# q, k and one more pair of gate chunks by Strassen's seven products, beside the attention

## The chip, the cores and the metric

The kernel runs on one core of one Trainium2 chip. A core has five engines, each with its own instruction stream: TensorE (PE, matmuls; PEld in a profile is its weight load), VectorE (DVE), ScalarE (ACT), GpSimd (POOL) and SyncE (SP, which here only issues DMAs). SBUF is the memory on chip with 128 partitions; PSUM has eight banks of 128 x 512 float32, into which TensorE accumulates. The metric is the device time in microseconds (us) of one execution.

## The reference, cut to what matters

One decoder layer for 256 rows of width 2048, 16 heads of 128 and a feed-forward width of 5632, all float32:

```python
h = rmsnorm(x, g_mix)
proj = h @ w_in                      # q, k, v of 16 heads (3 x 2048), then 3 x 2048 gate columns
q, k, v = ...
gates = sigmoid(proj[..., 3 * MIX_WIDTH:])
o_a = stick_breaking_attention(q[:, :4], k[:, :4], v[:, :4])
qn, kn = rmsnorm(q[:, 4:], q_gain), rmsnorm(k[:, 4:], k_gain)
o_b = moba_attention(qn[:, :6], kn[:, :6], v[:, 4:10], rel_bias)
o_c = dilated_attention(qn[:, 6:], kn[:, 6:], v[:, 10:], rel_bias)
merged = gates[0] * (o_a @ w_branch[:512]) + gates[1] * (o_b @ w_branch[512:1280]) \
       + gates[2] * (o_c @ w_branch[1280:])
x = x + merged @ w_out
gu = rmsnorm(x, g_ffn) @ w_gu
x = x + (silu(gu[..., :D_FF]) * gu[..., D_FF:]) @ w_down
```

With 256 rows, MoBA is causal softmax over one block, and the dilated attention is a softmax with a table of biases; so both are `softmax_pair` in the kernel.

## The kernel before

**Precision.** Every large product is done in three matmuls of a faster 32-bit format: a value is split into hi (ScalarE's copy, line 95) and lo (VectorE's subtraction, line 96), and `product` (149 to 152) adds hi*hi, hi*lo and lo*hi. Activations stand as columns of 128 x 128 (the stationary side), weights stream 512 columns wide. A block of weights, `w_raw` or `g_raw`, is two K tiles of 128 by 512 columns, 512 KB, and is split into `w_hi` and `w_lo`, of which there are four buffers each.

**A plain chunk** (`project`, 131) multiplies all 16 K tiles of h by 512 columns, for both row halves, into two PSUM banks `ps`.

**A pair** (`project_pair`, 301) does two chunks, colA and colB. In two of the four K chunks (`WC`) it uses Strassen's scheme: rows, K tiles and the two chunks each make the halves of a 2 x 2 block product, and `form` makes one of seven products, from sums of blocks of h (made once, `put_sums`) and of blocks of the weights (`u`, `add_into`, on VectorE). The other two K chunks are multiplied plainly (`rest`). It holds four PSUM banks: X and Y (`ps`), Z and V (from a second pool `acc2`). Results are put together with `snapshot` (ScalarE) and VectorE. `begin_pair` loads and splits the first blocks of the next pair while the present one ends.

**The order of the work.** h is made from x in `rest_of_x` while the first chunk runs. For each group of four heads q, k and v are three plain chunks, and the group's attention runs in the next group's chunks. This interleaving is by generators: `stages` and `slow_stages` hold functions that yield, and `advance` lets the first in the list do its next step; `project` advances both every second K tile, `parts` (a split in a pair) advances `stages`. `finish_stages` runs a list to its end. Behind the heads come twelve gate chunks: four plain, then four pairs, for which the attention's PSUM banks are given up and the sums of h are made (`sums_of_h`). Then w_branch, w_out, eleven pairs of w_gu, and w_down, whose pairs have their own code. Within each engine a planner of the framework fixes the order of instructions before the run, by a simulated timeline in which earlier program order has precedence; `keep_in_program_order` binds an instruction to the written order (all weight loads of pairs, on SP's queue, among others).

**What the softmax heads do:** q and k are scaled by the first norm (line 616), squared and summed per head on VectorE (619, 620), normalised (583), transposed (590 and following); the scores get the bias (542, 544), which stands in SBUF for all twelve heads, loaded once from a table `vec` in HBM (469).

Of the kernel before, what the change touches and what calls it, by code (L numbers as in the profile page):

```python
# [18 lines left out]
P = 128  # L19
# [36 lines left out]
def hybrid_block(ctx: ExitStack, tc: tile.TileContext, x, g_mix, w_in, q_gain, k_gain, w_branch, w_out,  # L56
# [7 lines left out]
    acc = ctx.enter_context(tc.tile_pool(name="acc", bufs=4, space=PSUM))  # L64
# [16 lines left out]
    hp_stack, h2_stack, ph1, pright = ExitStack(), ExitStack(), ExitStack(), ExitStack()  # L81
# [49 lines left out]
    def project(acts, k0, w, row0, nk, col0, fine=False, last=1):  # L131


        ps = [acc.tile([P, NB], F32, name="ps") for _ in range(NT)]
# [131 lines left out]
    def load(w, k, col0, pl=None):  # L266

        raw = pl.tile([P, 2, NB], F32, name="g_raw", bufs=8 if pl is gx else 4) if pl else wpool.tile([P, 2, NB], F32, name="w_raw", bufs=4)
        (nc.sync.dma_start if w is w_down else fetch)(raw, w[k * P:(k + 2) * P, col0:col0 + NB].rearrange("(k p) n -> p k n", p=P))
        return raw  # L270

    def parts(src):
# [3 lines left out]
        advance(stages)  # L276
        return hi, lo

# [12 lines left out]
    def begin_pair(acts, w, colA, colB):  # L291
# [6 lines left out]
        return p11, b12, u  # L298

    def project_pair(acts, w, colA, colB, begun=None, nxt=None):  # L300
# [23 lines left out]
        p11, b12, u = begun or begin_pair(acts, w, colA, colB)  # L324
# [50 lines left out]
    o = Columns(p1, "o", NH)  # L375
    h = Columns(pool(hp_stack, "hp", "left"), "h", KT)

    pa = pool(pat, "pa", "left", 2)
    zeros = pa.tile([P, NB], F32R, name="zeros", bufs=1)
# [33 lines left out]
    for t in range(NT):  # L413
        to_h(h, xs[0][t], 0, t, g1)
    idle(4)

    def rest_of_x():
        for c in range(1, 4):
            for t in range(NT):
# [5 lines left out]
        for c in range(4):  # L425
            squares(xs[c], ss1, c)
# [4 lines left out]
    stages.append(rest_of_x())  # L431
# [13 lines left out]
    oh_sb = pa.tile([N_BUCKETS, NDIST], F32, name="oh_sb", bufs=1)  # L445
    nc.gpsimd.dma_start(oh_sb, onehot)
    ex_sb = pa.tile([H_SOFT, NDIST], F32, name="ex_sb", bufs=1)
    nc.gpsimd.dma_start(ex_sb, extra)
    rb_sb = pa.tile([N_BUCKETS, H_SOFT], F32, name="rb_sb", bufs=1)
    nc.gpsimd.dma_start(rb_sb, rel_bias)  # L450
    bias = pa.tile([P, H_SOFT, S], F32, name="bias", bufs=1)

    def parameters():
# [7 lines left out]
        yield  # L461
        pb = tr.tile([P, 4 * P], F32, name="tr")
        nc.tensor.matmul(pb[:H_SOFT, :NDIST], rb_sb, oh_sb, start=True, stop=True)
        nc.vector.tensor_add(ex_sb, ex_sb, pb[:H_SOFT, :NDIST])
        vec = dram.tile([H_SOFT, NDIST], F32, name="vec")
        nc.gpsimd.dma_start(vec, ex_sb)
        yield
        for h in range(0, H_SOFT, 4):
            nc.gpsimd.dma_start(bias[:, h:h + 4, :], bass.AP(tensor=vec.tensor, offset=vec.offset + h * NDIST,
                                                             ap=[[1, P], [NDIST, 4], [1, S]]))  # L470
            yield
# [15 lines left out]
    def finish(h0, po):  # L487
        split(o.hi[:, h0:h0 + 2, :], o.lo[:, h0:h0 + 2, :], po)

    def stick_breaking(hl, qT, kT, v):  # L490
# [11 lines left out]
        sp = pa.tile([P, n], F32, name="sb_sp", bufs=1)  # L502
        nc.vector.scalar_tensor_tensor(sp, z[:, :n], 0.0, l, op0=ALU.max, op1=ALU.add)
        lb = pa.tile([P, n], F32, name="sb_lb", bufs=1)
# [27 lines left out]
    def softmax_pair(h0, hl, qT, kT, v):  # L532
        hs = h0 - H_A
# [3 lines left out]
        for i in range(2):  # L537
# [5 lines left out]
                             s[:, 0:W0].rearrange("p (h k) -> p h k", h=2), bias[:, hs:hs + 2, :])  # L543
        nc.vector.tensor_add(p[:, W0:n].rearrange("p (h k) -> p h k", h=2),
                             s[:, W0:n].rearrange("p (h k) -> p h k", h=2), bias[:, hs:hs + 2, P:S])
# [13 lines left out]
        pTs = []  # L559
        for i in range(2):  # L560
# [4 lines left out]
            pT = pa.tile([P, 3 * P], F32, name="sm_pT")  # L565
            nc.scalar.copy(pT.rearrange("p (b q) -> p b q", b=3),
                           backwards(pt[:, :3 * P].rearrange("p (b q) -> p b q", b=3)))
            pTs.append(pT)
# [10 lines left out]
    def rows_to_columns(g, j, sbs, dst, rr):  # L579
        for t in range(NT):  # L580
            if g:
                sb3 = sbs[t].rearrange("p (h d) -> p h d", h=4)
                nc.vector.tensor_mul(sb3, sb3, rr[:, 4 * t:4 * t + 4, None].to_broadcast([P, 4, HD]))
        yield
        yield
        for t in range(NT):
            yield
            pt = transpose4(sbs[t])
            d = dst[:, :, t * P:(t + 1) * P]
# [5 lines left out]
            else:  # L595
                nc.scalar.activation(d, pt, AF.Copy, scale=SCALE)

    def attention(g, qT, kT, v):
        for hl in (0, 2):
            if g:  # L600
                yield from softmax_pair(4 * g + hl, hl, qT, kT, v)
# [4 lines left out]
    for g in range(4):  # L606
        v = pa.tile([P, NT, NB], F32, name="v")
        qkT = [pa.tile([P, 4, S], F32, name=f"{n}T") for n in "qk"]
        for j in range(2):
            ps = project(h, 0, w_in, 0, KT, j * NH * HD + g * NB, fine=g + j == 0)  # L610
            finish_stages(stages)
            ss = pa.tile([P, 4 * NT], F32, name="ss")
            sbs = []
            for t in range(NT):
                sb = half_kb()
                nc.scalar.activation(sb, ps[t], AF.Copy, scale=rstd[:, t:t + 1])
                if g:
                    junk = half_kb()
                    nc.vector.tensor_mul(junk, sb, sb)
                    nc.vector.tensor_reduce(ss[:, 4 * t:4 * t + 4], junk.rearrange("p (h d) -> p h d", h=4),  # L620
                                            op=ALU.add, axis=AX.X)
                sbs.append(sb)
            rr = pa.tile([P, 4 * NT], F32, name="rr")
            if g:
                rsqrt_mean(rr, ss, HD, 4 * NT)
            stages.append(rows_to_columns(g, j, sbs, qkT[j], rr))
        ps = project(h, 0, w_in, 0, KT, 2 * NH * HD + g * NB)
        finish_stages(stages)
        finish_stages(slow_stages)
        for t in range(NT):  # L630
            nc.scalar.activation(v[:, t, :], ps[t], AF.Copy, scale=rstd[:, t:t + 1])
        slow_stages.append(attention(g, *qkT, v))


    gate_mem = dram.tile([3, 4, NT, P, NB], F32, name="gate_mem")

    def gate_col(c, b):
        return 3 * NH * HD + b * D + c * NB
# [7 lines left out]
    def sums_of_h(hs):  # L646
        for c in WC:
            w = gx.tile([P, 4, S], F32, name="u")
            k = slice(4 * c, 4 * c + 4)
            nc.vector.tensor_add(w, h.hi[:, k, :].bitcast(F32), h.lo[:, k, :].bitcast(F32))  # L650
            yield
            hs.put_sums(c, w[:, :, 0:P], w[:, :, P:S], w)
            yield

    chunks = [(c, b) for c in range(4) for b in range(3)]
    for c, b in chunks[:3]:
        keep_gate(c, b, project(h, 0, w_in, 0, KT, gate_col(c, b)))
    finish_stages(slow_stages)
    pat.close()

    acc2 = ctx.enter_context(tc.tile_pool(name="acc2", bufs=1, space=PSUM))
    pg2 = ExitStack()
    hs = Both(pool(pg2, "spg", "left"), h, WC)
    gx = pool(pg2, "gxg", "left", 3)
    stages.append(sums_of_h(hs))
    ps = project(h, 0, w_in, 0, KT, gate_col(*chunks[3]))
    ahead = begin_pair(hs, w_in, gate_col(*chunks[4]), gate_col(*chunks[5]))
    keep_gate(*chunks[3], ps)
    finish_stages(stages)
    for i in range(4, len(chunks), 2):  # L670
        one, two = chunks[i:i + 2]
        nxt = [(hs, w_in, *(gate_col(*cb) for cb in chunks[i + 2:i + 4]))] if i + 2 < len(chunks) else [None]
        g, ahead = project_pair(hs, w_in, gate_col(*one), gate_col(*two), ahead, *nxt)
        keep_gate(*one, g[:2])
        keep_gate(*two, g[2:])
    pg2.close()
    hp_stack.close()


# [244 lines left out]
```

## Time and profile before

| | |
|---|---|
| median of three executions | 1481.12 us (1481.09 to 1482.36) |
| the profiled execution | 1482.6 us, span 1480.8 us |
| mean granted TensorE clock | 0.997 |
| HBM read, written | 292.65 MB, 16.27 MB |
| first q chunk to the last v chunk | about 11 to 314 us |
| gate chunks | about 314 to 584 us |
| w_branch and w_out | to about 765 us |
| w_gu | to about 1222 us |

The span goes from the first to the last instruction; the execution's time has a little around it. A row of grouped instructions has the line, the engine, the operation, what it writes and reads, the count, then busy microseconds and the mean nanoseconds of one, then the idle time of the engine before them and what ended it. The busy time of TensorE is modelled for overlapping matmuls, so single gaps are read from starts.

### The profile page before, as it was taken

What the parts mean: (1) busy time and instruction counts of PE and PEld (TensorE: products, weight loads), DVE (VectorE), ACT (ScalarE), POOL (GpSimd) and SP (SyncE); (2) the same over time, 40 slices, a digit from 0 to 9 for tenths busy, and PEclk for the clock granted to TensorE, in tenths of its full rate; (3) what the DMA queues carried; (4) which work ended last, traced back from release to release, by engine and by line L of the source; (5) the groups of instructions that cost most, each with busy time, mean ns of one, the idle gap of its engine ahead of it and who ended that gap; (6) DMA issues with size and microseconds to landing.
All of it is one profiled execution on the core that took longest, in us unless ns stands there. A gap on an engine that the chain in (4) does not pass through costs nothing.

```text
span 1480.8 us, 17760 instructions
## 1 busy us (share of the span) xinstructions
PE 1469.1 (99%) x6467; PEld 1183.4 (80%) x6467; DVE 1135.7 (77%) x1228; ACT 817.5 (55%) x973; POOL 70.6 (5%) x130
## 2 busy tenths in 40 slices
PE   8999999999999999999999999999999999999998
PEld 6888888888887778888877888888888888888887
DVE  6457575754688887776779999998999888987675
ACT  5554454445466656344546666666656665664453
POOL 1000000000000001110000000000000000010000
PEclk9999999999999999999999999999999999999999
DMA  7655555556765566876776655566675557677553
GB/s 247 225 170 154 175 170 165 165 169 196 261 224 188 198 242 208 298 233 198 230 253 227 248 196 196 196 232 226 213 242 209 181 186 257 233 262 248 186 171 100
DMA packets 154425, 310.11 MB, mean 209 GB/s; under 512 B 10624, under 2 KB 12240, under 8 KB 154336
## 3 DMA queue, kind: packets, MB, share of 16 engines
q1 hardware_dynamic: 142624, 274.24, 55.5%
q0 software_dynamic: 9952, 32.62, 6.7%
q10 hardware_dynamic: 1760, 2.11, 0.4%
q8 instruction: 51, 0.84, 0.2%
q14 instruction: 38, 0.31, 0.1%
HBM read 292.65 MB, written 16.27 MB: 209 GB/s over the span
## 4 chain that ended last, share of the span: by engine, by line
PE 97%; DVE 1%; ACT 1%; DMA 1%; issue 0%; ACTq 0%; DVEq 0%
PE ps L151 23%; PE ps L152 23%; PE ps L150 23%; PE z L151 4%; PE z L152 4%; PE z L150 4%; PE v L150 3%; PE v L151 2%; PE v L152 2%; PE tr L172 2%; PE tr L150 1%; PE tr L152 1%; PE tr L151 1%; DVE w_lo L96 1%; DMA w_raw<-in_w_in 1%; ACT w_hi L95 0%
## 5 line engine op out<-in xcount | busy, mean ns | idle before, releaser
L96 DVE TENSOR_TENSOR w_lo<-w_raw,w_hi 128x1024 fp32r<-128x1024 f32 (+1 forms) x378 | 459.4, 1217 | 223.9 <-ACT w_hi L95 222.3
L95 ACT CAST w_hi<-w_raw 128x1024 fp32r<-128x1024 f32 (+1 forms) x378 | 394.8, 1046 | 394.7 <-PE ps L152 290.0
L152 PE MATMUL ps<-w_hi,h_lo 128*128 128x512 f32 x800 | 316.3, 396 | 0.0
L151 PE MATMUL ps<-w_lo,h_hi 128*128 128x512 f32 x800 | 316.2, 396 | 0.0
L150 PE MATMUL ps<-w_hi,h_hi 128*128 128x512 f32 x800 | 309.5, 399 | 0.8 <-ACT h_hi L95 0.8
L95 ACT CAST w_hi<-g_raw 128x1024 fp32r<-128x1024 f32 x144 | 150.6, 1049 | 96.7 <-PE ps L152 70.2
L96 DVE TENSOR_TENSOR w_lo<-g_raw,w_hi 128x1024 fp32r<-128x1024 f32 x144 | 173.6, 1223 | 36.1 <-ACT w_hi L95 34.0
L150 PEld LDWEIGHTS ps<-w_hi,h_hi 128*128 128x128 f32 x800 | 150.4, 188 | 36.4 <-ACT h_hi L95 1.5
L152 PEld LDWEIGHTS ps<-w_hi,h_lo 128*128 128x128 f32 x800 | 150.2, 188 | 36.3
L151 PEld LDWEIGHTS ps<-w_lo,h_hi 128*128 128x128 f32 x800 | 150.3, 188 | 35.8 <-DVE gq L459 0.6
L95 ACT CAST w_hi<-u 128x1024 fp32r<-128x1024 f32 x108 | 112.9, 1048 | 60.4 <-DVE u L286 53.5
L96 DVE TENSOR_TENSOR w_lo<-u,w_hi 128x1024 fp32r<-128x1024 f32 x108 | 129.5, 1222 | 14.5 <-ACT w_hi L95 13.9
L286 DVE TENSOR_TENSOR u<-u,g_raw 128x1024 f32<-128x1024 f32 x60 | 70.6, 1219 | 0.0
L150 PE MATMUL ps<-w_hi,o_hi 128*128 128x512 f32 x128 | 50.6, 399 | 0.0
L151 PE MATMUL ps<-w_lo,o_hi 128*128 128x512 f32 x128 | 50.6, 395 | 0.0
L152 PE MATMUL ps<-w_hi,o_lo 128*128 128x512 f32 x128 | 50.6, 395 | 0.0
L150 PE MATMUL ps<-w_hi,m_hi 128*128 128x512 f32 x128 | 50.5, 394 | 0.0
L152 PE MATMUL ps<-w_hi,a_lo 128*128 128x512 f32 x128 | 50.4, 394 | 0.0
L151 PE MATMUL ps<-w_lo,a_hi 128*128 128x512 f32 x128 | 50.4, 394 | 0.0
L152 PE MATMUL ps<-w_hi,m_lo 128*128 128x512 f32 x128 | 49.9, 390 | 0.0
L151 PE MATMUL ps<-w_lo,m_hi 128*128 128x512 f32 x128 | 49.8, 389 | 0.0
L281 ACT COPY sc<-ps 128x512 f32<-128x512 f32 x47 | 27.5, 584 | 38.3 <-PE ps L152 38.3
(307 smaller groups left out, 2433.4 us busy)
## 6 DMA issues: line engine op xcount, KB each, us to landing
w_raw<-in_w_in SPq DMA_DIRECT2D x158, 512.0 KB, 3.7
g_raw<-in_w_gu SPq DMA_DIRECT2D x88, 512.0 KB, 7.1
w_raw<-in_w_gu SPq DMA_DIRECT2D x88, 512.0 KB, 4.5
w_raw<-in_w_down SPq DMA_DIRECT2D x64, 512.0 KB, 4.6
g_raw<-in_w_in SPq DMA_DIRECT2D x32, 512.0 KB, 6.6
w_raw<-in_w_branch SPq DMA_DIRECT2D x32, 512.0 KB, 4.7
w_raw<-in_w_out SPq DMA_DIRECT2D x32, 512.0 KB, 4.7
g_raw<-in_w_down SPq DMA_DIRECT2D x24, 512.0 KB, 5.3
```

The source lines that it names most:

```text
L95: nc.scalar.copy(hi, src)
L96: nc.vector.tensor_sub(lo, src, hi.bitcast(F32))
L150: nc.tensor.matmul(ps, ah, wh, start=start, stop=False, **how)
L151: nc.tensor.matmul(ps, ah, wl, start=False, stop=False, **how)
L152: nc.tensor.matmul(ps, al, wh, start=False, stop=stop, **how)
L172: nc.tensor.transpose(pt[:, i, :], src[:, i * P:(i + 1) * P], ident)
L281: nc.scalar.copy(sb, ps)
L286: tc.keep_in_program_order(nc.vector.tensor_add(d, d, a))
```

## The change: what it does

1. The units of the input projection get a list of their own: v of group 0, gate chunk 0, then q and k of group 0 as one pair, q and k of group 1, v of group 1, and so on; gate chunk 1, then **five** pairs of gates. v and two gate chunks stay plain. Nine pairs of the input projection stand where there were four.
2. PSUM: `acc` has two names, `ps` and `qs`, of two banks each, used in turn (`banks`). A q/k pair takes all four (X, Y of one name, Z, V of the other), since the attention's banks are in use.
3. `wpool` has five buffers of `w_hi` and `w_lo` in place of four; `g_raw` has six in place of eight. `begin_pair` also loads and splits b21.
4. The sums of h are made inside `rest_of_x`, and the squares for the first norm are spread over it. `project` advances `stages` at every K tile; `parts` advances `slow_stages` at every second split.
5. To find the room: the attention's output is kept as float32 (`o_raw`) and split later, during the gate pairs; the bias is loaded per two heads; the tables' inputs go through the scratch pool and are loaded later; two tiles of the attention share a buffer, `v` has one.
6. The squares of q and k move to ScalarE, one instruction per head.
7. Behind: the early tiles of the down stage, its weight buffers and `a_raw` (two buffers) get other places in SBUF; the descriptor ring of POOL's DMAs is 4096 bytes.

```diff
-    acc = ctx.enter_context(tc.tile_pool(name="acc", bufs=4, space=PSUM))
+    acc = ctx.enter_context(tc.tile_pool(name="acc", bufs=2, space=PSUM))
...
-    wpool = pool(ctx, "wpool", "right", 4)
+    wpool = pool(ctx, "wpool", "right", 5)
     scratch = pool(ctx, "scratch", "right", 12)
+    gx = pool(pgx, "gx", "right", 2)
...
+    turn = ["ps", "qs"]
+    def banks():
+        turn.reverse()
+        return [acc.tile([P, NB], F32, name=turn[1]) for _ in range(2)]
...
         for k, w_hi, w_lo in weights(w, row0, nk, col0, fine):
+            if k:
+                advance(stages)
             if k % 2 == 0 and k:
-                advance(stages)
                 advance(slow_stages)
...
-        raw = pl.tile([P, 2, NB], F32, name="g_raw", bufs=8 if pl is gx else 4) ...
+        raw = pl.tile([P, 2, NB], F32, name="g_raw", bufs=6 if pl is gx else 4) ...
...
         split(hi, lo, src)
         advance(stages)
+        split_count[0] += 1
+        if split_count[0] % 2:
+            advance(slow_stages)
...
-        return p11, b12, u
+        b21 = quarter(acts, w, 1, colA)
+        return p11, b12, u, b21, [parts(b) for b in b21]
...
-        X = acc.tile([P, NB], F32, name="ps")
-        Y = acc.tile([P, NB], F32, name="ps")
-        Z = acc2.tile([P, NB], F32, name="z")
-        V = acc2.tile([P, NB], F32, name="v")
+        X, Y = banks()
+        Z, V = others()
...
         s1 = snapshot(X)
-        b21 = quarter(acts, w, 1, colA)
-        form(Y, 2, b21, True, False)
+        form(Y, 2, p21, True, False, True)
...
+    def rest_of_x(columns):
         for c in range(1, 4):
-            for t in range(NT):
-                to_h(h, xs[c][t], c, t, g1)
+            squares(xs[c - 1], ss1, c - 1)
+            hcs = [to_h(h, xs[c][t], c, t, g1) for t in range(NT)]
             if c < 3:
                 xs.append(load_x(c + 1, fetch))
             yield
+            if c - 1 in WC:
+                hs.put_sums(c - 1, *columns)
+            columns = hcs
             yield
...
+        oh_sb, ex_sb, rb_sb = (half_kb() for _ in range(3))
+        nc.gpsimd.dma_start(oh_sb[:N_BUCKETS, :NDIST], onehot)
+        nc.gpsimd.dma_start(ex_sb[:H_SOFT, :NDIST], extra)
+        nc.gpsimd.dma_start(rb_sb[:N_BUCKETS, :H_SOFT], rel_bias)
+        yield
+        yield
         pb = tr.tile([P, 4 * P], F32, name="tr")
...
     def finish(h0, po):
-        split(o.hi[:, h0:h0 + 2, :], o.lo[:, h0:h0 + 2, :], po)
+        nc.scalar.copy(o_raw[:, h0:h0 + 2, :], po)
...
+    def rows_to_columns(g, sbs, dst):
+        if g:
+            ss = pa.tile([P, 4 * NT * 2], F32, name="ss", bufs=1)
+            for i, sb in enumerate(sbs):
+                junk = half_kb()
+                for hd in range(4):
+                    cols = slice(hd * HD, (hd + 1) * HD)
+                    nc.scalar.activation(junk[:, cols], sb[:, cols], AF.Square,
+                                         accum_out=ss[:, 4 * i + hd:4 * i + hd + 1])
+                yield
+            rr = pa.tile([P, 4 * NT * 2], F32, name="rr", bufs=1)
+            rsqrt_mean(rr, ss, HD, 4 * NT * 2)
+            yield
...
     def attention(g, qT, kT, v):
+        biases = []
+        if g:
+            for hl in (0, 2):
+                bias = pa.tile([P, 2, S], F32, name="bias")
+                nc.gpsimd.dma_start(bias, bass.AP(tensor=vec.tensor, ...))
+                biases.append(bias)
...
+    def keep_v(g, ps):
+        finish_stages(slow_stages)
+        heads["v", g] = v = pa.tile([P, NT, NB], F32, name="v", bufs=1)
+        for t in range(NT):
+            nc.scalar.activation(v[:, t, :], ps[t], AF.Copy, scale=rstd[:, t:t + 1])
+        if g:
+            slow_stages.append(attention(g, *heads["qk", g], v))
+
+    def keep_qk(g, q0, q1, k0, k1):
+        sbs = []
+        for t, (src, own) in enumerate(((q0, True), (q1, False), (k0, True), (k1, True))):
+            sb = src if own else half_kb()
+            nc.scalar.activation(sb, src, AF.Copy, scale=rstd[:, t % NT:t % NT + 1])
+            sbs.append(sb)
+        heads["qk", g] = qkT = [pa.tile([P, 4, S], F32, name=f"{n}T") for n in "qk"]
+        if g:
+            stages.append(rows_to_columns(g, sbs, qkT))
+        else:
+            slow_stages.append(rows_to_columns(g, sbs, qkT))
+            slow_stages.append(attention(g, *qkT, heads["v", g]))
...
+    units = [("v", 0), ("gate", chunks[0]), ("qk", 0), ("qk", 1), ("v", 1), ("qk", 2), ("v", 2), ("qk", 3), ("v", 3)]
+    units += [("gate", chunks[1])] + [("gates", chunks[i:i + 2]) for i in range(2, len(chunks), 2)]
...
+    def in_turn():
+        turn.reverse()
+        return [acc.tile([P, NB], F32, name=turn[1]) for _ in range(2)]
+
+    def beside():
+        return [acc2.tile([P, NB], F32, name=n) for n in "zv"]
+
+    def split_o():
+        for k in range(0, NH, 4):
+            split(o.hi[:, k:k + 4, :], o.lo[:, k:k + 4, :], o_raw[:, k:k + 4, :])
+            yield
+            yield
...
+    others = in_turn
+    ahead = None
+    for (kind, what), after in zip(units, units[1:] + [(None, None)]):
+        if kind == "gates" and what[0] == chunks[4]:
+            finish_stages(slow_stages)
+            pat.close()
+            acc2 = ctx.enter_context(tc.tile_pool(name="acc2", bufs=1, space=PSUM))
+            others = beside
+            o = Columns(pool(ph1, "o", "left"), "o", NH)
+            stages.append(split_o())
+        nxt = pair_of(*after)
+        if kind in ("qk", "gates"):
+            ps, ahead = project_pair(*pair_of(kind, what), ahead, nxt)
+            if others is in_turn:
+                turn.reverse()
+        else:
+            ps = project(h, 0, w_in, 0, KT, 2 * NH * HD + what * NB if kind == "v" else gate_col(*what),
+                         fine=(kind, what) == ("v", 0))
+            ahead = begin_pair(*nxt) if nxt else None
+        finish_stages(stages)
...
+    pe = pool(ctx, "pe", "left")
...
+    pr = pool(ctx, "pr", "right")
+    gd = pool(ctx, "gd", "right", 4)
...
-        raw = pe.tile([P, 4, S], F32, name="a_raw", bufs=1)
+        raw = pr.tile([P, 4, S], F32, name="a_raw", bufs=2)
...
-    nc = bacc.Bacc("TRN2", target_bir_lowering=False, num_devices=1)
+    nc = bacc.Bacc("TRN2", target_bir_lowering=False, num_devices=1, dynamic_dma_scratch_size=4096)
```

More of the change, by code (lines that the diff above doesn't have):

```diff
@@ L429, in rest_of_x @@
         rsqrt_mean(rstd, sst, D, NT)
[L431 removed]
+    stages.append(rest_of_x(columns))
     before = pa.tile([P, P], F32, name="before", bufs=1)
@@ L443, in hybrid_block @@
     nc.gpsimd.memset(neg_ones, -1.0)
[L445 to L451, printed above, removed]
+    vec = dram.tile([H_SOFT, NDIST], F32, name="vec")
     def parameters():
@@ L461, in parameters @@
         yield
+        oh_sb, ex_sb, rb_sb = (half_kb() for _ in range(3))
[4 more added lines that the diff above has]
+        yield
         pb = tr.tile([P, 4 * P], F32, name="tr")
[L463 to L466, printed above, removed]
+        nc.tensor.matmul(pb[:H_SOFT, :NDIST], rb_sb[:N_BUCKETS, :H_SOFT], oh_sb[:N_BUCKETS, :NDIST], start=True, stop=True)
+        nc.vector.tensor_add(ex_sb[:H_SOFT, :NDIST], ex_sb[:H_SOFT, :NDIST], pb[:H_SOFT, :NDIST])
+        nc.gpsimd.dma_start(vec, ex_sb[:H_SOFT, :NDIST])
         yield
[L468 to L471, printed above, removed]
     stages.append(parameters())
@@ L658, in hybrid_block @@
[L658 to L675, printed above, removed]
@@ L676, in hybrid_block @@
-    pg2.close()
-    hp_stack.close()
+    others = in_turn
[18 more added lines that the diff above has]
+        finish_stages(stages)
+        if kind == "v":
+            keep_v(what, ps)
+        elif kind == "qk":
+            keep_qk(what, *ps)
+        elif kind == "gate":
+            keep_gate(*what, ps)
+        else:
+            keep_gate(*what[0], ps[:2])
+            keep_gate(*what[1], ps[2:])
```

124 lines of the change are left out of this document (45 added, 79 removed).

## The prediction

> **What bounds the kernel now.** I read the page first: the engines' busy time and the chain that ended last.
>
> ```profile
> PE 1469.1 (99%) x6467; PEld 1183.4 (80%) x6467; DVE 1135.7 (77%) x1228; ACT 817.5 (55%) x973; POOL 70.6 (5%) x130
> PE 97%; DVE 1%; ACT 1%; DMA 1%; issue 0%; ACTq 0%; DVEq 0%
> ```
>
> TensorE (PE) is busy 99% of the span and is 97% of the chain, so a matmul taken away should shorten the run, as long as nothing else becomes late. Next, the busy time by stretch: the start, three groups of four heads (q, k, v chunks with attention in between), one pair of gate chunks, and the w_gu stage.
>
> ```profile
> core 0: us, PE busy (x) PEld busy (x) DVE busy (x) ACT busy (x) POOL busy (x), PEclk, DMA share, GB/s
> 11.00:39.50 28.50, 28.50 (x125) 22.49 (x125) 21.32 (x33) 18.72 (x34) 0.52 (x1) 0.92 0.73 236
> 161.40:237.80 76.40, 76.40 (x354) 62.14 (x353) 48.72 (x77) 37.30 (x59) 0.00 (x0) 1.00 0.56 169
> 498.00:541.00 43.00, 42.61 (x182) 33.72 (x182) 37.63 (x35) 26.95 (x32) 2.24 (x5) 1.00 0.63 221
> 780.00:1222.00 442.00, 442.00 (x1937) 355.36 (x1938) 403.60 (x375) 280.86 (x314) 18.31 (x27) 1.00 0.61 213
> ```
>
> In the group of heads VectorE (DVE) has 27.7 of 76.4 us free. In w_gu, made of Strassen pairs alone, it works 403.6 of 442 us (91%) and TensorE never idles. The waits that TensorE does have come from one source:
>
> ```profile
> PE ps L151 <- DVE w_lo L96: 3.1, 5, 1.9
> PE z L151 <- DVE w_lo L96: 0.5, 3, 0.2
> ```
>
> The unit price of a matmul comes from the chain in order of time (start, length, what), and from single rows of the timeline:
>
> ```profile
> 449.94 0.70 PE ps L150 x3
> 457.45 1.24 DVE w_lo L96
> 462.46 1.06 ACT w_hi L95
> 463.55 1.24 DVE w_lo L96
> 492.86 0.70 PE ps L150 x3
> ...
> 893.63 0.70 PE ps L150 x3
> 936.51 0.70 PE ps L150 x3
> ```
>
> ```profile
> 454.91 0.39 PE L150 MATMUL ps<-w_hi,h_hi 128*128 128x512 f32 x1
> ...
> 457.71 0.39 PE L151 MATMUL ps<-w_lo,h_hi 128*128 128x512 f32 x1
> ```
>
> Three matmuls take 0.70 us on the chain, and twelve lie between starts at 454.91 and 457.71: 2.80 / 12 = **0.2333 us each** (the 0.39 is latency; they overlap). A gate pair recurs after 492.86 - 449.94 = 42.92 us. It has 180 matmuls, 42.0 us, so 0.9 us of it is waiting: the chain leaves TensorE at 457 and at 462 to 464. A w_gu pair recurs after 42.88 us, which eight transposes fill; it waits for nothing.
>
> **The change, part by part.**
>
> **The products.** Two chunks taken plainly are 2 x 16 K tiles x 2 row halves x 3 = 192 matmuls. A pair takes seven products in place of eight in two of four K chunks: 2 x 7 x 2 x 3 = 84, and 96 for the other two, 180. Five pairs are new (q and k of four groups, and one of gates), each replacing two plain chunks: 5 x 12 = 60 matmuls, 60 x 0.2333 = **-14.0 us**. All attention matmuls and transposes remain in number.
>
> The Trainium skill ("TensorE: Matmul & The Clock Gate", section Wait — 56ns, not 53.3ns?) gives 215.7 ns between warm matmuls of 512 columns; by that the saving would be an estimated 12.9 us. The trace's 0.2333 differs from it and I keep the trace.
>
> **What else the pairs ask of VectorE and ScalarE.** Grouped rows of the q/k/v stage (85 to 314 us, three groups): count, then busy us and mean ns of one, then the idle time before and its releaser.
>
> ```profile
> L96 DVE TENSOR_TENSOR w_lo<-w_raw,w_hi 128x1024 fp32r<-128x1024 f32 x73 | 89.4, 1224 | 69.0 <-ACT w_hi L95 69.0
> L619 DVE TENSOR_TENSOR sc<-sc 128x512 f32<-128x512 f32 x12 | 8.3, 688 | 3.1 <-ACT sc L616 3.1
> L620 DVE TENSOR_REDUCE ss<-sc 128x4 f32<-128x512 f32 x12 | 8.2, 685 | 0.3
> L95 ACT CAST w_hi<-w_raw 128x1024 fp32r<-128x1024 f32 x72 | 75.4, 1048 | 95.1 <-PE ps L152 93.7 <-issue 1.0
> L553 ACT ACTIVATE p<-p,sm_st 128x128 f32<-128x128 f32 x8 | 3.1, 388 | 0.0
> L553 ACT ACTIVATION_READ_ACCUMULATOR p<-p,sm_st 128x1 f32 x16 | 3.0, 187 | 0.0
> ```
>
> VectorE in one group now: 48.7, of which 24 splits x 1.224 = 29.4, so attention is 19.3. Squares and sums of q and k move to ScalarE (L619 and L620: 16.5 / 3 = 5.5 off), and the split of the attention's output moves behind it (2 of 0.69, 1.4 off): 12.4 left. New total: pair 37.6 + v chunk 8 x 1.224 = 9.8 + 12.4 = 59.8. TensorE in a group: 276 x 0.2333 = 64.4, and the attention's own 76.4 - 288 x 0.2333 = 9.2: 73.6. So VectorE is at 81%, under the 91% at which w_gu has no wait. ScalarE: 37.3 - 24 x 1.048 = 12.1 of attention, 16 squares of 128x128 at 0.388 + 0.187 = 9.2, pair 26.95 without its four sigmoids (2.8) 24.1, v 8.4: 53.8 of 73.6, 73%. No engine but TensorE is full; I put **0** for load. If that cover failed, the excess over 73.6 per group would be the price; none is left over.
>
> **Waits at the pairs' heads.** In gate pairs four sigmoids stand on ScalarE at the boundary before the next u's cast, and the 0.9 us follow. The new order splits b21 with b11 ahead of the pair, and the fifth buffer holds one more block, so forms 1 and 2 (24 matmuls, 5.6 us) now run before u is needed. On the other side nine pairs have heads, and q/k pairs put four scalings there. Three pairs pay 0.9 now (2.7). Bounds after: 0 (-2.7) to 9 x 0.9 (+5.4). I take half the price at each of nine, 4.1 - 2.7 = **+1.4**, since cover and crowding both grow.
>
> Two gate chunks among exp and log also mean more table loads:
>
> ```profile
> 337.31 1.28 ACT L643 ACT_TABLE_LOAD   x1
> 353.88 1.28 ACT L553 ACT_TABLE_LOAD   x1
> 362.32 1.28 ACT L643 ACT_TABLE_LOAD   x1
> ```
>
> These are three alternations where five would stand: +2 x 1.28 = 2.6 us of ScalarE, hidden by four blocks of split weights where they don't fall on a head. I take 0, bound +2.6, inside the +5.4. The Trainium skill ("ScalarE: Activation LUTs", What ACT_TABLE_LOAD costs) counts 2.66 us per switch with its drain: the bound would be an estimated 5.3, the sum the same while hidden.
>
> **Entry to w_gu.** The longest wait of the trace stands there:
>
> ```profile
> 767.88 0.47 PE L150 MATMUL ps<-w_hi,h_0hi 128*128 128x512 f32 x1
> 770.27 0.50 PE L151 MATMUL ps<-w_lo,h_0hi 128*128 128x512 f32 x1 [1.92 <-DVE w_lo L96]
> 764.54 0.63 ACT L399 ACTIVATE sc<-sc 128x512 f32<-128x512 f32 x1 [4.43 <-DVE sc L721]
> 766.71 1.03 ACT L95 CAST w_hi<-g_raw 128x1024 fp32r<-128x1024 f32 x1
> ```
>
> ScalarE idles 4.43 us, then squares, then casts b21, and TensorE loses 2.39 - 0.23 = 2.16 us. Begun ahead, and with a fifth buffer free, b21 can be cast in that idle time. Late next are the squares and the norm's few small operations, which nothing needs before the pair's end. Bounds -2.2 to +0.5 (a split more in front of the norm); I take **-1.5**.
>
> **The start.** The sums of h for K chunks 0 and 1 move from the gates into the first projection, and the bias tables' three loads move from the kernel's first microseconds to the middle of it, on the POOL queue, two steps (2 x 6 matmuls, 2.8 us) before a matmul that reads them.
>
> ```profile
> L193 DVE TENSOR_TENSOR u<-u 128x256 f32<-128x256 f32 x2 | 0.8, 418 | 0.0
> L96 DVE TENSOR_TENSOR h_lo<-sc,h_hi 128x512 fp32r<-128x512 f32 x8 | 5.4, 684 | 0.2 <-ACT h_hi L95 0.2
> oh_sb<-in_onehot POOLq DMA_DIRECT2D x1, 47.9 KB, 6.9
> bias<-vec POOLq DMA_DIRECT2D x3, 512.0 KB, 5.8
> ```
>
> Per chunk 4 x 0.42 + 2 x 0.684 = 3.0 us, 6.1 in all, on a VectorE that has 28.5 - 21.3 = 7.2 free there; one chunk's 3.0 may come ahead of a split that is needed. The matmul on the tables could wait 6.9 - 2.8 = 4.1 us if it is placed right behind its two steps. Bounds 0 to 7.1; splits run several blocks ahead and other matmuls can be placed first, so I take **+1.0**.
>
> **Refill of the pair's weights.** Six buffers for g_raw in place of eight: the next pair's b12 falls on b21's buffers, which are free only after the last addition.
>
> ```profile
> 1003.16 10.14 SPq L92 DMA_DIRECT2D g_raw<-in_w_gu  x8
> 1010.55 2.35 DVE L286 TENSOR_TENSOR u<-u,g_raw 128x1024 f32<-128x1024 f32 x2
> 1025.16 0.39 PE L151 MATMUL ps<-w_lo,h_0hi 128*128 128x512 f32 x1
> 1030.88 0.48 PE L150 MATMUL z<-w_hi,h_shi 128*128 128x512 f32 x1
> g_raw<-in_w_gu SPq DMA_DIRECT2D x88, 512.0 KB, 7.1
> ```
>
> Now all eight are asked for from 1003.16. Then b12 and, behind it in SP's order, b21 would be asked for from 1012.9 and land by 1020 to 1022 at 7.1 us each; b21 is used 2.8 us behind the first product of 1025.2, u at 1030.9. Some 5 us remain: **0**, bounds 0 to 0.45 for each of twenty pairs (+9), half of the wait that gate pairs have shown. The other moved pools touch stages in which TensorE never waits; a shorter descriptor ring could hold POOL up, which is busy 18.3 of 442 us and has as much time to wait: 0.
>
> **Sum:** -14.0 + 1.4 - 1.5 + 1.0 = -13.1. The profiled execution took 1482.6 us (span 1480.8 and 1.8 around it), 1.5 over the median of 1481.1; the difference is applied to the median: 1481.1 - 13.1 = **1468.0 us**.
>
> **The rivals.**
>
> *The waits vanish.* Earlier splits and a fifth buffer clear every head and the entry to w_gu, and the start costs nothing: -14.0 - 2.7 - 2.2 = -18.9, 1462.2 us. For it: w_gu pairs show no wait at 91%. Against: new work around each q/k head.
>
> *The refill is late.* If six buffers cost 0.45 us in each of twenty pairs: 1468 + 9 = 1477. For it: b12 and b21 queue behind a late release, and every later load behind them on SP. Against: 5 us of slack, worked out above.
>
> *Slower: VectorE is held by the bias.* The bias, resident before, is now fetched at the head of each group's attention, in the same step as the addition that reads it. VectorE runs in order, so behind a waiting addition stand all splits, and TensorE behind these. Price: issue 0.8 and landing 5.8, 6.6 us in each of three groups, 19.8 if nothing covers it: 1481.1 + 19.8 - 14.0 = 1487. It decides from 14.0 / 3 = 4.7 us exposed per group. For it: forms use a block in 6 x 0.2333 = 1.4 us, so five blocks ahead cover 7 us at best. Against: in the stage as it is VectorE waits 69 us in all for casts alone and TensorE never, and the addition may be placed later.
>
> **How the numbers follow.** Forecast 0.70, waits vanish 0.12, refill 0.09, bias 0.09. A measurement of this kernel tells about 0.2% (3.0 us) from no change. The refill, 4 us under today's time, may come a little dearer and fall inside that: 0.05 of it faster, 0.04 the same; of the bias 0.08 slower, 0.01 the same. Faster 0.70 + 0.12 + 0.05 = 0.87, same 0.05, slower 0.08. Range: from 1462, where every wait is gone, to 1475, where the unfavourable bounds of heads (+4.0 beyond what is taken) and part of the start come together; beyond lie the bias and most of the refill.
>
> **What would show it.** Right: TensorE's records fall by 60 (6467 to 6407), still at 0.2333; a q/k pair with its v recurs after some 74 us in place of 76.4; the wait at the entry to w_gu is gone; VectorE near 80% in the groups. Wrong: a TensorE wait on VectorE or ScalarE in each group that exceeds 2 us (bias), pairs of w_gu that recur after more than 42.9 us (refill), a first projection that ends late (start), or a matmul price other than 0.2333.

## The result, and the profile after

| | before | after |
|---|---|---|
| median | 1481.11 us | 1435.38 us (1435.01 to 1436.18) |
| span of the profiled execution | 1480.8 us | 1433.8 us |
| matmul instructions | 6467 | 6407 |

The ratio is 0.969, interval 0.9673 to 0.9707: 45.7 us faster. Forecast were 1468.0 us, 13.1 faster, with 1462 as the lower end. The direction was right, and the gain three and a half times as large as forecast.

The page of the kernel after: busy time of the engines, the shares of the chain that ended last (they add up to some 40%, since the chain could be followed back no further), one group of matmuls.

```profile
PE 1422.4 (99%) x6407; PEld 1173.4 (82%) x6407; DVE 1195.9 (83%) x1263; ACT 880.0 (61%) x1131; POOL 72.6 (5%) x133
...
PE 39%; DVE 1%; DMA 0%; issue 0%; ACT 0%; DVEq 0%; SPq 0%; ACTq 0%
...
L160 PE MATMUL ps<-w_lo,h_hi 128*128 128x512 f32 x368 | 144.1, 392 | 0.0
```

The 60 matmuls are gone, as counted. But busy PE time fell by 1469.1 - 1422.4 = 46.7 us, and 60 matmuls at 0.2333 are 14.0 of that. PE is still busy 99% of the span, so the rest isn't idle time that was closed: **the matmuls that are left became cheaper.** The mean of one matmul hides most of that: 392 ns here, and for the same product in the kernel before, in the view of groups,

```profile
L151 PE MATMUL ps<-w_lo,h_hi 128*128 128x512 f32 x800 | 316.2, 396 | 0.0
```

where both figures are latencies of matmuls that overlap. The price has to be read from starts. The timeline of TensorE after, in a gate pair:

```profile
439.92 0.39 PE L159 MATMUL v<-w_hi,h_hi 128*128 128x512 f32 x1
...
441.96 0.39 PE L159 MATMUL ps<-w_hi,b_shi 128*128 128x512 f32 x1
```

Nine starts follow each other in 2.04 us: **0.2267 us each, not 0.2333**. The mean granted clock is the same in both traces, 0.997 before and 0.998 after. The price of 0.2267 wasn't new: the kernel before had it in w_out, whose stationary tiles are `m`, and for 288 matmuls of w_down. Its timeline in w_out:

```profile
711.65 0.39 PE L151 MATMUL ps<-w_lo,m_hi 128*128 128x512 f32 x1
...
715.73 0.39 PE L151 MATMUL ps<-w_lo,m_hi 128*128 128x512 f32 x1
```

Eighteen starts in 4.08 us, 0.2267 each. So one kernel held both prices, for the same instruction in the same shape, at the same clock. What differs between the stages is where the stationary operand lies in SBUF. The byte addresses within a partition, from the two compiled programs:

```
                          before            after
w_hi, w_lo (streamed)     196576 = 224      188384 = 224    (modulo 256)
h_hi (stationary)          51744 =  32       23264 = 224
o_hi (stationary)          18976 =  32       72416 = 224
m_hi (stationary)         122848 = 224      114656 = 224
stationary minus streamed, modulo 256:
  64 bytes                5352 matmuls      none
   0 bytes                 672 matmuls      5964 matmuls
```

All that is allocated on SBUF's left side moved from 32 to 224 modulo 256. Two things shifted it: the shorter descriptor ring, by 12288 bytes, which is 48 x 256 and so changes nothing of this, and six small tiles of `rsqrt_mean` (three names, two buffers), which grew from 32 to 64 bytes each because the norm of the heads now does q and k in one call of 16 columns: 6 x 32 = 192 bytes. 224 - 32 = 192. Nothing in the change aims at this.

The other stretches, for comparison with those of before (start, a group of heads, a gate pair, w_gu):

```profile
core 0: us, PE busy (x) PEld busy (x) DVE busy (x) ACT busy (x) POOL busy (x), PEclk, DMA share, GB/s
0.00:36.00 36.00, 32.79 (x141) 25.52 (x142) 28.57 (x50) 24.40 (x44) 5.36 (x18) 0.95 0.82 266
170.00:245.00 75.00, 74.07 (x343) 61.15 (x342) 61.30 (x81) 51.32 (x100) 1.44 (x2) 1.00 0.57 185
440.00:482.00 42.00, 42.00 (x186) 34.52 (x185) 37.98 (x35) 27.76 (x32) 2.17 (x4) 1.00 0.67 228
760.00:1200.00 440.00, 438.50 (x1970) 362.29 (x1969) 408.28 (x383) 281.14 (x318) 19.30 (x29) 1.00 0.65 221
```

In w_gu 1970 instructions start in 440 us, 4.48 per us, where 1937 in 442 us were 4.38 before: 2.2% more. VectorE works 61.30 of 75 us in the group, 82%, ScalarE 51.32, 68%: about the load that was forecast (81 and 73%). The waits of TensorE:

```profile
PE tr L375 <- DVE sc L393: 1.5, 1, 1.5
PE tr L375 <- DVE sc L406: 1.4, 1, 1.4
PE qs L160 <- DVE w_lo L104: 1.4, 3, 0.8
PE ps L160 <- DVE w_lo L104: 1.1, 2, 0.8
PE ps L159 <- ACT v L645: 0.6, 1, 0.6
```

The first two belong to the start and were there before. The other three are 3.1 us in all; what the list has beyond them is 0.4 us or less, and no row of it names the bias or its tables.

### The profile page after: what moved, and what is told of

Its sections match the earlier page's. It is cut to its first block, busy times and chain, and to the rows that moved or that the text cites. A ratio compares the mean times of both kernels' runs of the same rounds, so it can differ in the third digit from the quotient of the medians.

```text
span 1433.8 us, 17776 instructions
## 1 busy us (share of the span) xinstructions
PE 1422.4 (99%) x6407; PEld 1173.4 (82%) x6407; DVE 1195.9 (83%) x1263; ACT 880.0 (61%) x1131; POOL 72.6 (5%) x133
## 2 busy tenths in 40 slices
DMA packets 154472, 310.09 MB, mean 216 GB/s; under 512 B 10672, under 2 KB 12288, under 8 KB 154384
## 5 line engine op out<-in xcount | busy, mean ns | idle before, releaser
L160 PE MATMUL ps<-w_lo,h_hi 128*128 128x512 f32 x368 | 144.1, 392 | 0.0
L161 PE MATMUL ps<-w_hi,h_lo 128*128 128x512 f32 x368 | 143.0, 390 | 0.0
L159 PE MATMUL ps<-w_hi,h_hi 128*128 128x512 f32 x368 | 140.4, 393 | 0.0
L160 PE MATMUL qs<-w_lo,h_hi 128*128 128x512 f32 x332 | 129.9, 391 | 0.8 <-DVE w_lo L104 0.8
L161 PE MATMUL qs<-w_hi,h_lo 128*128 128x512 f32 x332 | 129.4, 390 | 0.0
L159 PE MATMUL qs<-w_hi,h_hi 128*128 128x512 f32 x332 | 126.2, 391 | 0.0
L159 PEld LDWEIGHTS ps<-w_hi,h_hi 128*128 128x128 f32 x368 | 69.2, 188 | 15.1 <-ACT h_hi L103 1.1
L161 PEld LDWEIGHTS ps<-w_hi,h_lo 128*128 128x128 f32 x368 | 69.3, 188 | 14.2
L160 PEld LDWEIGHTS ps<-w_lo,h_hi 128*128 128x128 f32 x368 | 69.3, 188 | 14.0
L161 PEld LDWEIGHTS qs<-w_hi,h_lo 128*128 128x128 f32 x332 | 62.4, 188 | 12.8
```

The lines of the kernel that those rows point to most:

```text
L159: nc.tensor.matmul(ps, ah, wh, start=start, stop=False, **how)
L160: nc.tensor.matmul(ps, ah, wl, start=False, stop=False, **how)
L161: nc.tensor.matmul(ps, al, wh, start=False, stop=stop, **how)
```

## The experiments

**Theory A:** the address distance sets the price of a matmul, and 192 bytes moved it. **Rivals:** the price comes with the new order of instructions or with less pressure on some engine; or waits that the trace doesn't show as waits have gone.

**The price by itself.** A kernel that computes nothing of the reference and writes zeros: 128 groups of 24 matmuls, each group with one of eight offsets of the streamed tile and one of sixteen of the stationary tile.

```diff
+    for i in range(8):
+        for k in range(16):
+            ps = acc.tile([P, NB], F32, name="ps")
+            for n in range(N):
+                tc.keep_in_program_order(nc.tensor.matmul(ps, stat[k][n % 2], move[i][n // 2 % 2], ...))
```

> The kernel does none of the reference's work: it writes zeros to the output and runs 128 groups of 24 matmuls of 128x512, one group for each of 8 places of the streamed operand and 16 places of the stationary operand (byte address modulo 512, in steps of 32), with nothing else on the chip's engines. Theory A (the price of a matmul depends on where its two operands lie in SBUF): the groups fall into classes, with 0.2333 us from start to start where the stationary operand lies at 32 modulo 256 and the streamed one at 224, and 0.2267 where both lie at 224; other places may be dearer or cheaper. Rival B (the price comes from the accumulators' banks, the split buffers or the neighbours' traffic, and not from addresses): all 128 groups have one price.

The whole took 730.46 us. Its timeline of TensorE, with the streamed tile `mc` at 64 modulo 256 and stationary tiles `sb` to `sl` at 32, 64, ... 352 (start, time until the last end, what):

```profile
198.53 5.76 PE L88 MATMUL ps<-mc,sb 128*128 128x512 f32 x24
204.13 5.61 PE L88 MATMUL ps<-mc,sc 128*128 128x512 f32 x24
209.58 5.75 PE L88 MATMUL ps<-mc,sd 128*128 128x512 f32 x24
...
237.58 5.67 PE L88 MATMUL ps<-mc,si 128*128 128x512 f32 x24
243.09 5.76 PE L88 MATMUL ps<-mc,sj 128*128 128x512 f32 x24
248.68 5.61 PE L88 MATMUL ps<-mc,sk 128*128 128x512 f32 x24
254.13 5.75 PE L88 MATMUL ps<-mc,sl 128*128 128x512 f32 x24
```

`sc` and `sk` lie at distance 0 modulo 256: from 204.13 to the next group at 209.58 are 5.45 us, 0.227 each. `sb`, `sd` to `sh`, `sj` take 5.60, 0.233; `si`, at distance 192, takes 5.51, 0.230. Over all 128 groups but the first, which ran before the clock was full, the mean time between starts by distance:

```
(stationary - streamed) mod 256      ns from start to start
  0                                  226.7 to 226.8 (one group 228.0)
192                                  228.7 to 229.3
32, 64, 96, 128, 160, 224            232.4 to 234.1
```

Nothing else varies in this kernel, so the distance alone makes the two prices that the kernels show.

**The same addresses without the change, and the change without the addresses.** Two kernels, one line each, ahead of all other constants: 192 unused bytes in the kernel before, and 64 in the kernel after, which put the left side back to 32 modulo 256.

```diff
+    shift = consts.tile([P, 48], F32, name="shift"); nc.gpsimd.memset(shift, 0.0)   # the kernel before
+    shift = consts.tile([P, 16], F32, name="shift"); nc.gpsimd.memset(shift, 0.0)   # the kernel after
```

> The kernel before with an unused tile of 192 bytes per partition ahead of all others, so that every tile on the left side of SBUF lies 192 bytes further; the order of the instructions on every engine is the same but for one memset on POOL. Theory A: h, o and most of a, which lay at 32 modulo 256, come to lie at 224 like the weights; the 5352 matmuls on them fall from 0.2333 to 0.2267 us: 1481 - 35.7 = about 1445 us. Rival B: no effect, 1481 us.

1451.92 us (1451.31 to 1454.41), ratio 0.9806 with the interval 0.9791 to 0.9821, against 1481.46 there: **192 unused bytes are worth 29.5 us.**

> The changed kernel with an unused tile of 64 bytes per partition ahead of all others, which brings its left side from 224 back to 32 modulo 256, where the kernel before had it. Theory A: the 5580 matmuls on left tiles rise from 0.2267 to 0.2333 us: 1435.4 + 37 = about 1472 us, near the forecast of 1468. Rival B: no effect, 1435 us.

1465.84 us (1465.78 to 1465.98), ratio 0.9897, 0.988 to 0.9913: **30.6 us lost by 64 unused bytes.** The order of instructions is that of the parent on every engine in both, but for the memset; that excludes the rival of order. TensorE's timeline in the kernel after with 64 bytes:

```profile
439.79 0.40 PE L159 MATMUL ps<-w_hi,h_hi 128*128 128x512 f32 x1
...
445.15 0.39 PE L159 MATMUL z<-w_hi,b_shi 128*128 128x512 f32 x1
```

23 starts in 5.36 us: 0.2330 again. The price explains the size, too. 5580 matmuls (all but those on `m`) x 6.67 ns are 37.2 us; the 30.6 that were lost are 6.6 less. The rest is lateness: take the time from each matmul of a product to the next start on TensorE, subtract its price, and sum over the trace. That makes 17.9 us after and 10.9 with 64 bytes, 7.0 less, since waits shrink when matmuls are dearer. The other way round, the kernel before has 22.5 us with its cheaper matmuls in place of 15.4, since the casts and subtractions didn't become faster. Its waits with 192 bytes:

```profile
PE ps L151 <- DVE w_lo L96: 3.5, 5, 1.9
...
PE z L151 <- DVE w_lo L96: 1.0, 3, 0.3
PE v L150 <- ACT w_hi L95: 0.9, 2, 0.7
```

The z row was 0.5 and the v row wasn't there. This is most of why 1445 was missed: a cheaper matmul gives part of its gain back as waits.

**The products.** q and k of each group as two plain chunks again, everything else as after:

```diff
-            sb = src if own else half_kb()
+            sb = half_kb()
...
+        if kind == "qk":
+            ps = [*project(h, 0, w_in, 0, KT, what * NB), *project(h, 0, w_in, 0, KT, NH * HD + what * NB)]
+            ahead = begin_pair(*nxt) if nxt else None
...
```

> The changed kernel with q and k of the four groups as two plain chunks each instead of one pair: 4 x 12 = 48 matmuls more, operands at the same relative place (0 modulo 256), so at 0.2267 us each. Theory A (a pair is worth its twelve matmuls and costs nothing beside): 1435.4 + 10.9 = 1446.3 us. Rival B (the q/k pairs' VectorE work and their heads eat part of the saving): less than 1441. Rival C (the pairs are worth more than their matmuls, which would leave less to the addresses): 1455 or more.

1446.13 us (1442.11 to 1447.88), 0.9753, 0.9727 to 0.9779, beside 1435.24 for the kernel after: 10.9 us for 48 matmuls, 0.227 each, though single executions lie from 1442 to 1448. The late starts of the two traces agree, too: 17.4 us here, 17.9 in the kernel after. In sum the pairs bring just their products, and their heads cost no more than the plain chunks do.

**The fifth buffer.** `wpool` with four in the kernel after:

```diff
-    wpool = pool(ctx, "wpool", "right", 5)
+    wpool = pool(ctx, "wpool", "right", 4)
```

> The changed kernel with four buffers of w_hi and w_lo instead of five; all operands stay at the same relative place. Theory A (the fifth buffer is what keeps the heads of the pairs and the entry to w_gu free of waits, as the prediction has it): 0.9 us at nine heads and 2.2 at the entry come back, up to 10.3, about 1445 us. Rival B (splitting b21 ahead of the pair does it alone): 1435 to 1437.

1455.26 us (1453.18 to 1464.45), 0.9833, 0.9795 to 0.987: 20.0 us, twice the most that was expected. The waits of TensorE with four:

```profile
PE v L159 <- ACT w_hi L103: 2.9, 4, 1.4
PE tr L159 <- ACT w_hi L103: 2.3, 1, 2.3
PE qs L159 <- ACT w_hi L103: 2.0, 3, 1.1
...
PE z L159 <- ACT w_hi L103: 1.2, 1, 1.2
```

These are waits for casts, which hardly occur with five. Late starts grow from 17.9 to 33.3 us, 15.4 of the 17.6 by which this trace is longer. The reading, argued from the code and these rows: `begin_pair` now splits b11 and b21, two blocks each, while the present pair still runs. They fill four buffers, and the pair's last blocks find none. The gate pairs show it too: in three of them, TensorE comes late by 0.48 and 0.53 us with four buffers, and not with five.

Two things go with it that the expectation didn't have. After the waits near 398 and 1238 us the granted clock stands at one half for 3.4 us, and matmuls start 0.427 us apart:

```profile
402.00:406.00 4.00, 4.00 (x12) 3.13 (x12) 2.83 (x4) 1.78 (x3) 0.00 (x0) 0.57 0.90 333
```

That is 3.4 x (1 - 0.227 / 0.427) = 1.6 us each time, 3.2 of the 15.4, and the executions differ in their clock: 1453.18 us at a mean clock of 0.997, 1464.45 at 0.992. And with four buffers the planner also arrives at another order: in the two traces TensorE, ScalarE and VectorE do the same instructions in a different sequence from about 20 us on. No run separates the buffer from the order that comes with it.

**Both at once.** Is the fifth buffer worth 20 us by itself? In the kernel before with 192 bytes, five buffers and the short ring:

```diff
+    shift = consts.tile([P, 48], F32, name="shift"); nc.gpsimd.memset(shift, 0.0)
-    wpool = pool(ctx, "wpool", "right", 4)
+    wpool = pool(ctx, "wpool", "right", 5)
-    nc = bacc.Bacc("TRN2", target_bir_lowering=False, num_devices=1)
+    nc = bacc.Bacc("TRN2", target_bir_lowering=False, num_devices=1, dynamic_dma_scratch_size=4096)
```

> The kernel before with its left side 192 bytes further, a fifth buffer of w_hi and w_lo, and the descriptor ring of 4096 bytes that makes room for it; no new pairs. All matmuls at 0.2267 us. Theory A (at the cheaper matmul four buffers are too few, and the fifth takes back the waits of the shifted kernel): it stands above the changed kernel by the five pairs alone, 60 x 0.2267 = 13.6: about 1449 us. Rival B (the buffer helps only with the new order of splits): 1452, as without it.

1448.53 us (1447.15 to 1450.38), 0.9777, 0.9764 to 0.9791: only 3.4 us. And the kernel after with 64 bytes and four buffers, both edits as above:

> The changed kernel at the old price of a matmul (left side at 32 modulo 256) with four buffers. Without the fifth buffer it lost 20 us at the cheaper price. Theory A (TensorE at 0.2333 leaves the split engines more time, so the buffer is worth less there): 1465.8 + 5 to 10, 1471 to 1476 us. Rival B (it is worth the same at both prices): 1485 us.

1480.74 us (1475.47 to 1488.67), 0.9994, 0.9978 to 1.0009. **With neither the address nor the fifth buffer, the new order and its 60 saved matmuls bring nothing that can be measured.** The value lay between those of the two theories, 14.9 us for the buffer at the dearer matmul. Here, too, the executions spread with the clock, from 1475.47 us at 1.000 to 1488.67 at 0.996. All corners:

| matmul price | buffers | before's order | new order |
|---|---|---|---|
| 0.2333 | 4 | 1481.5 | 1480.7 |
| 0.2333 | 5 | not run | 1465.8 |
| 0.2267 | 4 | 1451.9 | 1455.3 |
| 0.2267 | 5 | 1448.5 | 1435.2 |

Read down: the address is worth 25 to 31 us in every column. Read across: the new order gains 13.3 us with five buffers; with four it gains 0.7 at one price and loses 3.4 at the other.

**The refill of w_gu.** Seven buffers of g_raw in the w_gu stage in place of six (eight don't fit there now):

```diff
-        raw = pl.tile([P, 2, NB], F32, name="g_raw", bufs=6 if pl is gx else 4) ...
+        raw = pl.tile([P, 2, NB], F32, name="g_raw", bufs=g_bufs[0] if pl is gx else 4) ...
...
-    split_count = [0]
+    split_count, g_bufs = [0], [6]
...
-    gx = pool(h2_stack, "gx2", "left", 2)
+    gx = pool(h2_stack, "gx2", "left", 2); g_bufs[0] = 7
```

> The changed kernel with seven g_raw buffers in the w_gu stage instead of six (eight don't fit). Theory A (the three waits of 1.0, 0.6 and 0.5 us in the first w_gu pairs are late refills): they shrink or go, 1433.3 to 1435 us. Rival B (they come from the order of VectorE and ScalarE at the entry): no change, 1435.4 us.

1433.17 us (1432.06 to 1433.44), 0.967, 0.9655 to 0.9685, 2.1 below the kernel after, with the same order of instructions on TensorE, ScalarE and VectorE. In the kernel after, SP's timeline shows the refill as it was argued (start, time until the last of eight is issued):

```profile
757.44 18.03 SPq L100 DMA_DIRECT2D g_raw<-in_w_gu  x8
...
799.46 18.78 SPq L100 DMA_DIRECT2D g_raw<-in_w_gu  x8
```

Eight loads are asked for over 18 us, where it took 10.14 before: the last two stand until a buffer is free, and every later load behind them. TensorE then waits at 787, 830 and 872 us, 1.03 + 0.56 + 0.51 = 2.1 us, in three pairs of eleven; in the list after they are the row of `ps` and part of that of `qs`, both for w_lo. With seven buffers the row of `ps` is gone, that of `qs` is shorter, and no wait is left at these three places:

```profile
PE qs L160 <- DVE w_lo L104: 1.0, 2, 0.8
PE ps L159 <- ACT v L645: 0.6, 1, 0.6
```

**The squares.** Those of q and k back on VectorE:

```diff
-                for hd in range(4):
-                    cols = slice(hd * HD, (hd + 1) * HD)
-                    nc.scalar.activation(junk[:, cols], sb[:, cols], AF.Square, ...)
+                nc.vector.tensor_mul(junk, sb, sb)
+                nc.vector.tensor_reduce(ss[:, 4 * i:4 * i + 4], junk.rearrange("p (h d) -> p h d", h=4), ...)
```

> The changed kernel with the squares and sums of q and k back on VectorE, as in the kernel before (5.5 us more on VectorE and 9.2 less on ScalarE in each of three groups). Theory A (VectorE has room in the groups, 59.8 + 5.5 of about 73 us, 89%): within 1 us of 1435.4. Rival B (VectorE's place in the queue ahead of the splits is what matters): each group loses 2 us or more, 1441 us or more.

1434.93 us (1432.58 to 1436.52), 0.9683, 0.9662 to 0.9705: no difference from the kernel after. VectorE has room in the groups.

**The kernel after again,** unchanged, on the chip of three other runs: the old order with five buffers, the new one with 64 bytes and four buffers, and the version below.

> The changed kernel once more, as the mark for the runs beside it on the same chip: 1435 us.

1435.24 us (1434.79 to 1438.28), 0.9692, 0.9679 to 0.9705; the kernel before had 1481.71 there. The differences above are against this value. The other runs of the whole kernel were on another chip, where the kernel before had 1481.46 or 1482.21, within half a microsecond of that.

**A version that beats both.** Seven buffers of g_raw as above, and a second one for `v`, whose single one made `keep_v` hold the next chunk's bank (the 0.6 us of `ACT v L645`):

```diff
-        heads["v", g] = v = pa.tile([P, NT, NB], F32, name="v", bufs=1)
+        heads["v", g] = v = pa.tile([P, NT, NB], F32, name="v", bufs=2)
```

> The changed kernel with seven g_raw buffers in the w_gu stage and a second buffer of v, which lets v of group 1 be written while the attention of group 0 still reads its own. Theory: the refill waits (2.1 us) and the wait on v near 182 us (0.85 us) are gone: 1432 to 1433 us. Rival: the attention's order changes and moves the wait elsewhere, 1433 to 1435.

1430.72 us (1429.98 to 1433.81), 0.966, 0.9647 to 0.9674: 4.5 below the kernel after, and its row of waits for `v` is gone. The two waits account for 2.95; where the other 1.5 come from wasn't followed.

## Why the prediction was wrong

**The step that failed** is "60 x 0.2333" together with "still at 0.2333": the unit price was taken as a constant of the instruction. It is one of the address, and it fell for the 5292 of the remaining matmuls whose distance changed. That is some 30 of the 45.7 us: 29.5 by the 192 bytes, and 30.6 by the 64, which also make 288 matmuls of w_down dear that were cheap before. No rival held it; a matmul price other than 0.2333 was named only among the things that would make the prediction wrong. The trace of before had the hint: twelve starts were measured in a gate pair, and a second such measurement in w_out would have given 0.2267. The Trainium skill ("TensorE: Matmul & The Clock Gate", section Wait — 56ns, not 53.3ns?) counts 215.7 ns for 512 columns; neither price here is that, the best being 226.7, and the section makes no difference by where the operands lie.

**The rest was nearly right.** At the old price, the change is worth 1481.46 - 1465.84 = 15.6 us (12.9 to 17.8 by the interval), where 13.1 were forecast. By terms, from the traces of the kernel before and of the kernel after with 64 bytes:

- **Products, -14.0:** shown, by the 60 records and by 10.9 us for 48 of them.
- **Load, 0:** shown, by 82% and by the squares, which can go on either engine.
- **Heads, +1.4:** too dear. At the old price, the three gate pairs that paid 0.9 us each pay 0.1, and the first gate pair, which is new, pays 1.1: -1.3. One q/k pair pays, too: at 186 us a matmul waits for the bank that the copy to `v` still reads, and 0.9 us are lost around it. That is -0.4 in all. "Cover and crowding both grow" named the two elements and weighed them alike; cover won by a little. What was missed altogether is that this cover hangs on the fifth buffer, or on the order that the planner finds with it: with four, the new kernel loses what the products gain.
- **Entry to w_gu, -1.5:** the 2.16 us and the 0.63 behind it are gone, -2.8.
- **Start, +1.0:** right, as far as single traces tell. The two traces can't be compared directly here, since the granted clock differs (the kernel before, then the kernel after with 64 bytes):

```profile
0.00:50.00 50.00, 45.76 (x189) 35.23 (x190) 29.86 (x49) 27.66 (x46) 7.68 (x21) 0.93 0.75 248
0.00:36.00 36.00, 32.33 (x140) 24.45 (x141) 28.57 (x49) 24.03 (x44) 5.42 (x19) 1.00 0.82 267
```

  The 128th matmul of a product starts at 46.5 us in the one and at 44.1 in the other. The kernel before with 192 bytes has the old order at a full clock (1.00 between 9 and 40 us), and starts its 128th at 42.3; 128 x 6.67 ns = 0.9 us for the old price make 43.2. So the new order is 0.9 us later, and 46.5 - 43.2 = 3.3 us are the clock of that one execution. The wait for the tables does occur:

```profile
PE tr L477 <- DMA sc<-in_rel_bias: 1.1, 1, 1.1
```

- **Refill, 0:** right at the price it was made for: with 64 bytes one pair of w_gu waits, 0.2 us. At 0.2267 it is 2.1 us in three pairs, by the mechanism of the rival, which took 9 over twenty: the slack of 5 us was counted in dearer matmuls, the splits became no faster, and the last two loads come later.
- **Bias:** no wait on it in the kernel after, at either price. From one copy of v to the next (182.4 to 255.6) a group takes 73.2 us with 279 matmuls; 279 x 0.2267 + 9.2 of attention are 72.4, and the rest is the wait for the bank of `v` just behind 182.4. So the group runs at TensorE's pace.

The two spans at the old price, 1480.8 and 1464.2, differ by 16.6: products -14.0, heads -0.4, entry -2.8, start +0.9, refill +0.2, the 288 matmuls of w_down that the 64 bytes make dear +1.9, and the clock at the start -3.3 are -17.5; the 0.9 that is left, spread over transposes, attention and small waits, wasn't followed. That 13.1 came so close to what the change is worth at the old price is partly luck: heads and entry were 3.1 us too dear together, and what had no term in the sum, w_down and the rest, nearly makes up for it.

## What to carry to other kernels

Read the time between matmul starts in several stages of one trace, not in one: where two stages with the same shape and clock differ by a few per cent, look at the operands' addresses. Any edit that changes the size of a small early tile can shift everything behind it, so before a change of some per cent is put down to what it does, pad it back to the old addresses and run that. A scheme that begins work ahead needs its buffers counted together with it: at the cheaper price the fifth buffer alone brought 3.4 us and the new order alone nothing, both together 16.7. And before a gap between two traces is put down to a term, compare the granted clock in that stretch: here it made 3.3 us of a difference of 16.6.

## What the runs showed of the hardware

A matmul of 128 x 512 that changes its stationary operand each time takes 226.7 ns from start to start when stationary and streamed operand are at the same byte address modulo 256, 228.7 to 229.3 when the stationary one lies 192 bytes on, and 232.4 to 234.1 at the six other multiples of 32 (128 combinations; the operands there were zeros, and the whole kernels, with data, have the same two prices). Why 0 and 192 differ from the rest isn't known from these runs, nor what happens at distances that aren't multiples of 32. In whole kernels, 192 bytes of padding were worth 29.5 us of 1481.5, 2%.

Behind waits of TensorE near 398 us (about 2.1 us in three pieces) and 1238 us (2.3 us), the granted clock of the kernel after with four buffers stood at one half for 3.4 us, and a matmul took 0.427 us from start to start. Not every wait is followed by that: behind the 2.16 us at 768 us in the kernel before, the clock stayed full.
